# Hybrid encoder block on one core: order of the first row blocks and scales, and GpSimd's share of the beginning moved to VectorE

## The chip, the core and the metric

The kernel runs on one core of a Trainium2 chip. The metric is the device time of one execution in microseconds, from runs of the whole program. The engines of the core, as the profile names them: PE (TensorE, matmuls; PEld its weight loads), DVE (VectorE), ACT (ScalarE), POOL (GpSimd) and SP (SyncE, which here only issues DMAs). Each engine works through its own instructions in the order in which the program gives them, and waits on semaphores where an operand comes from another engine or a DMA.

## The reference

One layer of an encoder block on 1024 tokens of width 1024, in f32. The part that matters here is the beginning:

```python
u = rms_norm(x, norm1_g[l])
proj = u @ w_in[l]
q, k, v, cb, cc, ch, ga, gb = jnp.split(proj, split_pts, axis=-1)
q = rms_norm(q.reshape(B, S, N_HEADS, HEAD_DIM), q_norm_g[l])
k = rms_norm(k.reshape(B, S, N_HEADS, HEAD_DIM), k_norm_g[l])
...
y_a = neighbourhood_attention(q, k, v, rpb[l]) @ w_attn_branch[l]
y_b = short_gated_conv(cb, cc, ch, conv_w[l]) @ w_conv_branch[l]
merged = jax.nn.sigmoid(ga) * y_a + jax.nn.sigmoid(gb) * y_b
x = x + merged @ w_o[l]
h = rms_norm(x, norm2_g[l]) @ w_mlp_in[l]
x = x + jnp.square(jax.nn.relu(h)) @ w_mlp_out[l]
```

V, Q and K have 512 columns each; the row norm is over the 1024 columns of x.

## The kernel before

**Numbers.** Products of f32 matrices are made from f16 halves: an operand is scaled by a power of two, rounded to f16 (the high part) and the rest is rounded again (the low part). A product takes three passes, high by high, high by low and low by high (`PASSES`, L440). So each weight chunk needs a scale, then high parts on ScalarE (L290, a copy with a scale) and low parts (L278 on VectorE, one multiply-and-subtract). For the scale, a chunk is measured once: V's two chunks by the largest magnitude, weighted by the row gain (`largest`, L296, VectorE), the chunks of Q, K, the convolution and the first gate by a sum of squares (L241, ScalarE, the squares themselves go to the place where the low parts will stand) times `gm2`, the squared largest row gain. A matmul with a matrix of ones (`all_sum`, L179) sums over the partitions, and a few 128x1 integer instructions make the power of two (`pow2`, L105, or `pow2_half`, L402).

**Row blocks.** x is eight blocks of 128 rows. `norm` (L414) is a generator, one step per yield: Square with its row sum and a root on ScalarE, four small VectorE instructions (`rstd`), the high half `u` on ScalarE (L420), the low half on VectorE (L422). Blocks 0 to 2 are then turned on TensorE (`ln_trans`: high and low half, each copied out of PSUM, L432 on ScalarE and L434 on VectorE), blocks 3 to 7 by a transposing DMA (`ln_turn`, L437). A turned block is an operand `uT` of every projection.

**Units.** A unit is 24 matmuls into one PSUM bank. `v_unit(b, j, steps, ticks)` (L502) makes half j (256 columns) of V for row block b, or both halves (512 columns) if j is None; its result is taken out later as two f16 halves (L508, L509). Behind a unit, `step` advances the generators of the foreground (`fg`) and `tick` those of the background (`bg`, the weight chunks that are being prepared). `apart` holds a generator back until some units more have been issued; it is a matter of order only. `flush` runs the background to its end.

**V's parts on GpSimd.** V's chunks have two pieces of 4 x 256 columns. The low parts of the first are made on VectorE, those of the second on GpSimd (`pool`): four scalings into f32 (L287), then four subtractions (L276).

**Gate forms.** The gates are computed later by a seven-product scheme. Its operands of the rows are made in this stage by `sforms` (L467), four times, for the block pairs (n, n + 4): two scalings of x on ScalarE (L474), four 512-column sums or differences on GpSimd (L480), the high half on ScalarE (L482, 2048 columns), the low half on VectorE (L484), and a store to DRAM (`sform_store`, L489). The f16 tile `s16` has two buffers, so the third form is written where the first stood until its store had read it. `SFORM` says after which unit each form starts.

**Weight loads.** There are five `raw` buffers. `load_upto` (L212) issues the next load as soon as a piece's low parts have been issued, and the load itself waits on SP's queue until these have run. All DMAs of this stage, loads, transposes and stores, are issued by SP in one order.

**The order.** The calls from L514 to L561 are written out by hand: which norm step, which tick and which unit come when. The loop `for p in range(11)` issues the rest of V (p 1 to 5 halves, p 6 to 10 whole blocks 3 to 7) and the norms of the later blocks; at p = 3 Q's chunk goes into the background. Q's eight units and K's eight follow (L611 on): each result is taken out of PSUM, scaled and normed by head (`qk_vec`: L577, L578 on ScalarE, L581 to L597 on both), and K's weight parts are made during Q's last units.

Of the kernel before, what the change touches and what calls it, by code (L numbers as in the profile page):

```python
# [52 lines left out]
def encoder_block(ctx: ExitStack, tc: tile.TileContext, x, weights, cols, gqk, rel, masks, out):  # L53
# [12 lines left out]
    def bank(tag):  # L66
        return psum.tile([128, 512], F32, name="ps_" + tag, tag=tag, bufs=banks[tag])
# [6 lines left out]
    def anybank():  # L74
        rc[0] += 1
        return bank("dsodsods"[rc[0] % 8])
# [83 lines left out]
    def apart(mark, n=3, of=units):  # L160
        while of[0] < mark + n and not forced[0]:
            yield WAIT
# [15 lines left out]
    def all_sum(a, out, bk, floor, lag=1):  # L178
        T.matmul(bk[:, 0:1], ones[:, 0:128], a, start=True, stop=True)  # L179
        yield  # L180
        yield from apart(units[0], lag)
        V.tensor_scalar(sc[:, out], bk[:, 0:1], floor, None, op0=OP.max)
        yield
# [16 lines left out]
    def settle():  # L200
        while late:
            late.pop(0)()
# [17 lines left out]
    class Chunk:  # L220


        def __init__(self, kind, widths, tag, rows, half, more):
            self.kind, self.bank = kind, {"V": "o", "Q": "o", "K": "s", "C": "d"}.get(kind)
            self.tag, self.rows, self.widths, self.more = tag, rows, widths, more
            self.offs = []
            self.raw, self.ready, self.half, self.pool = [], more > 0, half, () if half is None else (1,)
            self.split = False

        def prep(self):  # L230
            n = len(self.widths)
            nk = sum(k for k, _ in self.widths)
            rm, a, b, s = (cols_of("prep", i) for i in (nk, 1, 1, 1))
            self.inv = keep()
            tot = sum(k * w for k, w in self.widths)
            if self.kind in "QKCG":
                self.parts = wsp.tile([128, 2, tot], F16, name="w16_ws", tag="ws")
                for p, (k, w) in enumerate(self.widths):
                    while len(self.raw) <= p:
                        yield WAIT  # L240
                    A.activation(self.parts[:, 1, :k * w].bitcast(BF16), self.raw[p][:, :k * w], AF.Square,  # L241
                                 accum_out=sc[:, at(rm, p)])
                    yield
                V.tensor_reduce(sc[:, a], sc[:, at(rm, 0, n)], axis=AX, op=OP.add)
                c = ones_col()
                V.tensor_tensor(c, sc[:, a], sc[:, gm2], op=OP.mult)
                yield from apart(units[0], 2 if self.kind == "Q" else 3)
                yield from all_sum(c, b, bank(self.bank) if self.bank else anybank(), 1e-36)
                yield from pow2_half(b, 14, s, self.inv, more=self.more)
            else:  # L250
                yield from self.largest(rm, a, b)
                yield from pow2(b, 14, s, self.inv, False, more=self.more)
            V.tensor_scalar(sc[:, rm], sc[:, self.rows], sc[:, s], None, op0=OP.mult)
            yield
            while done[0] < self.first or self.tag not in wpool:
                yield WAIT
            if self.half is not None:
                if not self.half:
                    vhome.append(wsp.tile([128, 2, 2, tot], F16, name="w16_v", tag="ws"))
                self.parts = vhome[0][:, self.half]  # L260
            elif self.kind not in "QKCG":
                self.parts = wpool[self.tag].tile([128, 2, tot], F16, name="w16_" + self.tag, tag=self.tag)
            f = o = 0
            todo = []
            for p, (k, w) in enumerate(self.widths):
                todo.append((p, [(i * w, w, rm.start + o + i) for i in range(k)], f))
                f += k * w
                o += k
            prev, scaled = None, {}
            for it in todo + [None]:  # L270
                if prev:
                    p, parts, f = prev
                    for o, m, c in parts:
                        hi, lo = (self.parts[:, w, f + o:f + o + m] for w in range(2))
                        if p in self.pool:
                            G.tensor_tensor(lo, scaled[p][:, o:o + m], hi, op=OP.subtract)  # L276
                        else:
                            V.scalar_tensor_tensor(lo, self.raw[p][:, o:o + m], sc[:, c:c + 1], hi,  # L278
                                                   op0=OP.mult, op1=OP.subtract)
                    done[0] += 1  # L280
                    load_upto(done[0] + 5)
                if it:
                    p, parts, f = it
                    if p in self.pool:
                        scaled[p] = w1p.tile([128, 1024], F32, name="scaled", bufs=1)
                        for o, m, c in parts:
                            G.tensor_scalar(scaled[p][:, o:o + m], self.raw[p][:, o:o + m], sc[:, c:c + 1], 1.0,  # L287
                                            op0=OP.mult, op1=OP.mult)
                    for o, m, c in parts:
                        A.activation(self.parts[:, 0, f + o:f + o + m], self.raw[p][:, o:o + m], AF.Copy,  # L290
                                     scale=sc[:, c:c + 1])
                prev = it
                self.split = it is None
                yield
# [129 lines left out]
    def ln_trans(u16, b, dst):  # L424
        for s in range(2):
            pt = bank16("o")
            for k in range(8):
                T.transpose(pt[:, k * 128:(k + 1) * 128], u16[:, s, k * 128:(k + 1) * 128], ident)
            o = dst[:, s, :, b * 128:(b + 1) * 128]
            i = pt.rearrange("p (k t) -> p k t", k=8)  # L430
            if s == 0:
                A.activation(o, i, AF.Copy)  # L432
            else:
                V.tensor_copy(o, i)  # L434
# [27 lines left out]
    GS = dram.tile([128, 4, 4, 2, 512], F16, name="gs")  # L462

    turned, formed = [0], [0]
    SFORM = (6, 8, 10, 12)

    def sforms():  # L467

        for n, start in enumerate(SFORM):
            yield from apart(start, 0)  # L470
            assert turned[0] >= n + 5
            z = []
            for b in (n, n + 4):
                A.activation(xt[:, b], xt[:, b], AF.Copy, scale=sc[:, at(ys, b)])  # L474
                z += [xt[:, b, :512], xt[:, b, 512:]]
            f = wqk.tile([128, 4, 512], F32, name="sform", bufs=1)
            v = wqk.tile([128, 4, 2, 512], F16, name="s16", bufs=2)
            for o, a, b, op in ((2, z[0], z[2], OP.subtract), (0, z[2], z[3], OP.subtract),
                                (1, f[:, 0], z[0], OP.subtract), (3, z[1], f[:, 1], OP.add)):
                G.tensor_tensor(f[:, o], a, b, op=op)  # L480
            yield from apart(start, 2)
            A.activation(v[:, :, 0], f, AF.Copy)  # L482
            yield
            V.tensor_tensor(v[:, :, 1], f, v[:, :, 0], op=OP.subtract)  # L484
            fg.append(sform_store(n, v))
# [6 lines left out]
    def ln_step(b, n=1):  # L492
        for _ in range(n):
            advance(ln[b])
# [17 lines left out]
                               for k in range(8) for sa, sw in PASSES]), post, steps, ticks)  # L512

    push(cV[0])  # L514
    ln_step(0, 2)
    tick()
    ln_step(0, 5)
    ln_step(1)
    tick(3)
    ln_step(0)  # L520
    ln_step(1)
    tick(4)
    ln_trans(u16[:, 0], 0, UT)
    flush()
    ln_step(1, 5)
    ln_step(1)
    ln_step(2, 2)
    push(cV[1])
    tick(1)
    v_unit(0, 0, 0, 0)  # L530
    ln_step(2, 4)
    ln_trans(u16[:, 1], 1, UT)
    ln_step(2, 1)
    tick(3)
    ln_step(2)
    tick(4)
    ln_step(3, 2)
    ln_trans(u16[:, 2], 2, UT)
    ln_step(3, 4)
    fg.append(qk_gain())  # L540
    fg.append(sforms())
    V.tensor_reduce(sc[:, gm2], sc[:, g1], axis=AX, op=OP.max, apply_absolute_value=True)
    mul(gm2, gm2, gm2)
    for p in range(11):
        if p == 3:
            flush()
            push(cQ)
        if 0 < p < 6:
            v_unit(p % 3, p // 3, 1, 2)
        elif p:  # L550
            v_unit(p - 3, None, 2, 4)
        for q in (p,) if p < 6 else (2 * p - 6, 2 * p - 5):
            c = q // 2 + 3
            if c < 8 and q % 2 == 0:
                ln_step(c, 2)
                ln_turn(u16[:, c % 4], c, UT)
                turned[0] = c + 1
            if c < 7:
                ln_step(c + 1, 3)
    settle()  # L560
    flush()  # L561

# [1154 lines left out]
```

## Time and profile before

| | us |
|---|---|
| median of 3 runs | 1249.16 |
| lowest and highest | 1244.13, 1250.89 |
| profiled execution: time | 1249.31 |
| profiled execution: span of the core | 1247.2 |
| mean granted clock of TensorE | 0.992 |

The profile comes from one execution. A row of the timeline is: start, duration, engine, line of the kernel, operation, output<-inputs, shapes, count, and in brackets how long the engine had been idle before it and what released it. Neighbouring instructions of one kind are merged into one row (x24), whose duration runs from the first start to the last end. A row of the stretches is: the stretch, its length, then busy time and count for PE, PEld, DVE, ACT and POOL, the granted TensorE clock, the DMA engines' busy share, and GB/s. A row of the groups is: line, engine, operation, tiles, shapes, count, then busy us in total and mean ns of one, then the idle time before them and what ended it. Rows of one view that stand together are told apart by this form. "DMA to landing" is the time from the issue of a tile's DMAs to their completion.

| engine, whole span | busy us |
|---|---|
| PE | 1203.7 |
| DVE | 929.7 |
| ACT | 765.1 |
| POOL | 438.8 |

### The profile page before, as it was taken

What the parts mean: (1) busy time and instruction counts of PE and PEld (TensorE: products, weight loads), DVE (VectorE), ACT (ScalarE), POOL (GpSimd) and SP (SyncE); (2) the same over time, 40 slices, a digit from 0 to 9 for tenths busy, and PEclk for the clock granted to TensorE, in tenths of its full rate; (3) what the DMA queues carried; (4) which work ended last, traced back from release to release, by engine and by line L of the source; (5) the groups of instructions that cost most, each with busy time, mean ns of one, the idle gap of its engine ahead of it and who ended that gap; (6) DMA issues with size and microseconds to landing.
All of it is one profiled execution on the core that took longest, in us unless ns stands there. A gap on an engine that the chain in (4) does not pass through costs nothing. (4 is left out here: it accounts for less than half of the span.)

```text
span 1247.2 us, 17068 instructions
## 1 busy us (share of the span) xinstructions
PE 1203.7 (97%) x6294; PEld 577.4 (46%) x6294; DVE 929.7 (75%) x1733; ACT 765.1 (61%) x1177; POOL 438.8 (35%) x297
## 2 busy tenths in 40 slices
PE   4989999998999999999998999999999999999998
PEld 3534444554444444444456444444444444444444
DVE  6668778878557686887867655554546999999997
ACT  5777567677464454536665867877855773645430
POOL 2340002221231111101002756556557463373562
PEclk8999999999999999999998999999999999999999
DMA  6458455656552211216185445544575743436202
GB/s 256 105 191 182 79 119 136 130 104 136 122 112 83 68 52 51 68 38 251 59 164 115 155 164 162 186 146 134 186 264 182 272 191 134 173 112 240 101 34 101
DMA packets 170803, 173.35 MB, mean 139 GB/s; under 512 B 131424, under 2 KB 131936, under 8 KB 166624
## 3 DMA queue, kind: packets, MB, share of 16 engines
q1 hardware_dynamic: 170720, 172.27, 46.9%
q8 instruction: 49, 0.80, 0.3%
q14 instruction: 34, 0.28, 0.1%
HBM read 102.51 MB, written 37.75 MB: 112 GB/s over the span
## 5 line engine op out<-in xcount | busy, mean ns | idle before, releaser
L188 PEld LDWEIGHTS <-ops 128*128 128x128 f16 x1356 | 132.4, 98 | 159.3 <-issue 2.4
L188 PEld LDWEIGHTS <-w 128*128 128x128 f16 x1368 | 133.1, 98 | 143.8 <-issue 5.2
L858 PE MATMUL ps_d<-uT,w_ws 128*128 128x512 f16 x528 | 126.5, 382 | 0.0
L188 PE MATMUL ps_d<-ops 128*128 128x512 f16 (+1 forms) x528 | 118.3, 374 | 0.0
L188 PE MATMUL ps_s<-ops 128*128 128x512 f16 x492 | 113.2, 379 | 1.5 <-DVE ops L1550 1.1
L1541 ACT ACTIVATE ops<-hf,sc 128x2048 f16<-128x2048 f32 x26 | 52.0, 1999 | 94.6 <-PE ps_o L188 35.1
L1155 POOL TENSOR_TENSOR as<-as 128x512 f32<-128x512 f32 x64 | 88.0, 1374 | 42.5 <-ACT as L1412 38.7
L188 PEld LDWEIGHTS <-uT 128*128 128x128 f16 x648 | 64.8, 101 | 70.8 <-issue 5.7
L962 POOL TENSOR_TENSOR tsum<-raw 128x512 f32<-128x512 f32 x28 | 47.4, 1709 | 137.0 <-ACT raw L948 137.0
L188 PEld LDWEIGHTS <-w_s 128*128 128x128 f16 x588 | 56.7, 98 | 69.4 <-DVE w_s L973 1.9
L188 PE MATMUL ps_d<-u2x,w 128*128 128x512 f16 (+1 forms) x360 | 80.0, 372 | 0.0
L1543 DVE SCALAR_TENSOR_TENSOR ops<-hf,sc,ops 128x2048 f16<-128x2048 f32 x26 | 73.8, 2838 | 5.2 <-ACT ops L1541 5.2
L188 PE MATMUL ps_o<-ops 128*128 128x512 f16 x336 | 77.1, 379 | 0.0
L858 PEld LDWEIGHTS <-w_ws 128*128 128x128 f16 x528 | 51.2, 98 | 53.5 <-issue 1.7
L188 PE MATMUL ps_o<-u2T,w 128*128 128x512 f16 (+1 forms) x324 | 73.2, 376 | 0.0
L948 ACT ACTIVATE raw<-raw,sc 128x256 f32<-128x256 f32 x172 | 71.1, 493 | 0.9 <-DMA raw<-in_weights 0.9
L962 POOL TENSOR_TENSOR gsum<-raw 128x512 f32<-128x512 f32 x14 | 19.0, 1374 | 131.5 <-issue 57.1
L1436 DVE TENSOR_TENSOR as<-ps_d,as 128x512 f32<-128x512 f32 (+1 forms) x15 | 10.1, 674 | 62.5 <-ACT as L1453 62.5
L977 ACT ACTIVATE w<-raw,sc 128x512 f16<-128x512 f32 (+1 forms) x28 | 24.6, 927 | 52.2 <-DVE sc L410 52.2
L805 ACT ACTIVATE sz<-sz,sc 128x384 f32<-128x384 f32 (+1 forms) x64 | 37.3, 583 | 27.6 <-DVE sc L796 16.2
L188 PE MATMUL ps_s<-u2T,w 128*128 128x512 f16 (+1 forms) x252 | 52.7, 359 | 0.0
L278 DVE SCALAR_TENSOR_TENSOR w_ws<-raw,sc,w_ws 128x512 f16<-128x512 f32 (+2 forms) x72 | 49.0, 733 | 3.7 <-ACT w_ws L290 3.7
(333 smaller groups left out, 2616.3 us busy)
## 6 DMA issues: line engine op xcount, KB each, us to landing
raw<-in_weights SPq DMA_DIRECT2D x89, 512.0 KB, 5.6
hs<-as SPq DMA_DIRECT2D x16, 1792.0 KB, 8.8
hf<-hs SPq DMA_DIRECT2D x26, 1024.0 KB, 6.7
w2x<-in_weights SPq DMA_DIRECT2D x16, 512.0 KB, 8.1
raw<-in_weights SPq DMA_DIRECT2D x16, 384.0 KB, 3.9
xt<-in_x SPq DMA_DIRECT2D x8, 512.0 KB, 10.2
gs<-s SPq DMA_DIRECT2D x4, 1024.0 KB, 6.7
x<-in_x SPq DMA_DIRECT2D x8, 512.0 KB, 9.7
```

What stands on the lines that cost most here:

```text
L188: T.matmul(ps, l, r, start=a, stop=b)
L278: V.scalar_tensor_tensor(lo, self.raw[p][:, o:o + m], sc[:, c:c + 1], hi, op0=OP.mult, op1=OP.subtract)
L805: A.activation(z, z, AF.Exp, scale=-1.0, bias=sc[:, d["mx"]], accum_out=sc[:, d["sm"]])
L858: T.matmul(ps, l, r, start=a, stop=b)
L948: A.activation(v, v, AF.Copy, scale=sc[:, at(g, 4 * i + k)])
L962: G.tensor_tensor(t[:, o], a, b, op=OP.add)
L977: A.activation(o(0), w, AF.Copy, scale=sc[:, s])
L1155: sub.tensor_tensor(z[o], z[a], z[b], op=op)
L1436: V.tensor_tensor(z[5], ps[6], z[4], op=OP.add)
L1541: A.activation(P[:, 1, 0], hf, AF.Copy, scale=sc[:, Rs])
L1543: V.scalar_tensor_tensor(P[:, 1, 1], hf, sc[:, Rs], P[:, 1, 0], op0=OP.mult, op1=OP.subtract)
```

## The change

It touches the beginning only, up to the last block of V. The second chunk of V (`half` = 1) gets its scale from sums of squares, like Q and K, without the waits of order, and writes its squares into its own place in V's tile; `gm2` is therefore made earlier. GpSimd no longer makes low parts of V, and the sums of the gate forms go to VectorE. The written order is changed: norm 0 is finished up to its high half ahead of V's first measurement, norm 1's small instructions come ahead of V's parts, block 1's unit for the first half of V comes before block 2 is turned, and in the last rounds (p 6 to 10) the foreground advances behind the norms instead of behind the unit, with more ticks of the background. The first form starts after unit 7 instead of 6, and its second part one unit sooner.

```diff
@@ class Chunk @@
-            self.raw, self.ready, self.half, self.pool = [], more > 0, half, () if half is None else (1,)
+            self.raw, self.ready, self.half = [], more > 0, half
@@ prep @@
-            if self.kind in "QKCG":
-                self.parts = wsp.tile([128, 2, tot], F16, name="w16_ws", tag="ws")
+            if self.kind in "QKCG" or self.half:
+                self.parts = vhome[0][:, 1] if self.half else wsp.tile([128, 2, tot], F16, name="w16_ws", tag="ws")
...
-                yield from apart(units[0], 2 if self.kind == "Q" else 3)
-                yield from all_sum(c, b, bank(self.bank) if self.bank else anybank(), 1e-36)
+                if not self.half:
+                    yield from apart(units[0], 2 if self.kind == "Q" else 3)
+                yield from all_sum(c, b, bank(self.bank) if self.bank else anybank(), 1e-36, not self.half)
...
-            prev, scaled = None, {}
+            prev = None
...
-                        if p in self.pool:
-                            G.tensor_tensor(lo, scaled[p][:, o:o + m], hi, op=OP.subtract)
-                        else:
-                            V.scalar_tensor_tensor(lo, self.raw[p][:, o:o + m], sc[:, c:c + 1], hi,
-                                                   op0=OP.mult, op1=OP.subtract)
+                        V.scalar_tensor_tensor(lo, self.raw[p][:, o:o + m], sc[:, c:c + 1], hi,
+                                               op0=OP.mult, op1=OP.subtract)
...
-                    if p in self.pool:
-                        scaled[p] = w1p.tile([128, 1024], F32, name="scaled", bufs=1)
-                        for o, m, c in parts:
-                            G.tensor_scalar(scaled[p][:, o:o + m], self.raw[p][:, o:o + m], sc[:, c:c + 1], 1.0,
-                                            op0=OP.mult, op1=OP.mult)
@@ sforms @@
-    SFORM = (6, 8, 10, 12)
+    SFORM = (7, 8, 10, 12)
...
-                G.tensor_tensor(f[:, o], a, b, op=op)
-            yield from apart(start, 2)
+                V.tensor_tensor(f[:, o], a, b, op=op)
+            yield from apart(start, 1)
@@ the written order @@
     push(cV[0])
-    ln_step(0, 2)
+    ln_step(0, 7)
     tick()
-    ln_step(0, 5)
     ln_step(1)
     tick(3)
     ln_step(0)
     ln_step(1)
     tick(4)
     ln_trans(u16[:, 0], 0, UT)
+    ln_step(1, 4)
+    V.tensor_reduce(sc[:, gm2], sc[:, g1], axis=AX, op=OP.max, apply_absolute_value=True)
+    mul(gm2, gm2, gm2)
     flush()
-    ln_step(1, 5)
+    ln_step(1)
     ln_step(1)
     ln_step(2, 2)
     push(cV[1])
-    tick(1)
+    tick(2)
     v_unit(0, 0, 0, 0)
     ln_step(2, 4)
     ln_trans(u16[:, 1], 1, UT)
     ln_step(2, 1)
-    tick(3)
+    tick(1)
+    v_unit(1, 0, 0, 0)
+    tick(7)
     ln_step(2)
-    tick(4)
-    ln_step(3, 2)
+    ln_step(3, 1)
     ln_trans(u16[:, 2], 2, UT)
-    ln_step(3, 4)
+    tick(2)
+    ln_step(3, 5)
     fg.append(qk_gain())
     fg.append(sforms())
-    V.tensor_reduce(sc[:, gm2], sc[:, g1], axis=AX, op=OP.max, apply_absolute_value=True)
-    mul(gm2, gm2, gm2)
     for p in range(11):
         if p == 3:
             flush()
             push(cQ)
-        if 0 < p < 6:
+        if p == 1:
+            step()
+            tick(2)
+        elif p and p < 6:
             v_unit(p % 3, p // 3, 1, 2)
-        elif p:
-            v_unit(p - 3, None, 2, 4)
+        elif p > 5:
+            v_unit(p - 3, None, 0, 4 if p < 7 else 8)
...
                 ln_step(c + 1, 3)
+        if p > 5:
+            step(2)
     settle()
     flush()
```

In the order in which the changed program gives its instructions, SP's DMAs of this stage stand as follows behind the last transposing DMA of `uT`: before, the store of form 0, four weight loads (K's pieces 1 to 3 and the convolution's first), the stores of forms 1 to 3; after, the four weight loads, then the stores of forms 0 to 3.

## The prediction

> **What bounds the kernel now.** The page first: is there one bound, and where is it absent?
>
> ```profile
> span 1247.2 us, 17068 instructions
> PE   4989999998999999999998999999999999999998
> ```
>
> TensorE is the bound almost everywhere; the first three slices (31 us each) are the weak ones. The change touches only instructions up to the first block of K, so I read that stretch in order of time, TensorE first.
>
> ```profile
> 24.36 0.18 PE L179 MATMUL ps_o<-ones 128*128 128x1 bf16 x1 [3.54 <-DVE ones L311]
> 26.45 4.29 PE L188 MATMUL ps_s<-w_v,uT 128*128 128x256 f16 x24
> 36.53 2.78 PE L188 MATMUL ps_s<-w_v,uT 128*128 128x256 f16 x24
> 65.01 5.35 PE L188 MATMUL ps_s<-w_v,uT 128*128 128x512 f16 x24 [2.34 <-DMA uT<-u]
> 75.81 3.24 PE L188 MATMUL ps_d<-w_ws,uT 128*128 128x512 f16 x14 [0.87 <-DVE w_ws L278]
> 78.89 5.34 PE L188 MATMUL ps_o<-w_ws,uT 128*128 128x512 f16 x24
> 115.17 5.34 PE L188 MATMUL ps_d<-w_ws,uT 128*128 128x512 f16 x24
> 120.35 5.34 PE L188 MATMUL ps_o<-w_ws,uT 128*128 128x512 f16 x24
> ...
> 24.00:26.00 2.00, 1.42 (x13) 1.23 (x14) 1.86 (x7) 0.20 (x2) 0.00 (x0) 0.50 0.02 8
> 100.00:120.00 20.00, 20.00 (x95) 9.05 (x93) 18.39 (x49) 15.51 (x26) 1.83 (x2) 1.00 0.76 133
> ```
>
> Three losses stand here: 3.54 us for V's second scale, after which the granted clock is 0.50 and a unit of 24 matmuls takes 4.29 instead of 2.78; 2.34 us for row block 7; and some 3.4 us in Q's first unit, which follows block 7's (65.01 + 5.35), waits for its weight parts until 75.81, and ends when the next begins, at 78.9: 8.5 us for 5.2. From then TensorE never stops, one 512-column unit each 5.18 us (115.17 to 120.35, the first of K). But in 100 to 120 VectorE is busy 18.39 of 20 us: the lead it has there is small, and that decides this case.
>
> **The durations.** One row each for the operations that the change adds, removes or moves (mean of one in ns; POOL's forms row is one of three):
>
> ```profile
> L422 DVE SCALAR_TENSOR_TENSOR u<-xt,sc,u 128x1024 f16<-128x1024 f32 x8 | 11.7, 1461 | 7.0 <-ACT u L420 5.8 <-DMA xt<-in_x 1.2
> L484 DVE TENSOR_TENSOR s<-sform,s 128x2048 f16<-128x2048 f32 x4 | 9.2, 2288 | 8.1 <-ACT s L482 8.1
> L301 DVE TENSOR_REDUCE sc<-raw 128x4 f32<-128x1024 f32 x4 | 4.9, 1215 | 0.7 <-DMA raw<-in_weights 0.6
> L509 DVE SCALAR_TENSOR_TENSOR vT<-ps_s,vT 128x512 f16<-128x512 f32 x3 | 2.0, 679 | 0.0
> L588 DVE TENSOR_TENSOR qs<-qs,sc 128x512 f32<-128x512 f32 x2 | 1.4, 686 | 0.0
> L420 ACT ACTIVATE u<-xt,sc 128x1024 f16<-128x1024 f32 x8 | 9.2, 1144 | 5.3 <-DVE sc L399 5.2
> L474 ACT ACTIVATE xt<-xt,sc 128x1024 f32<-128x1024 f32 x8 | 8.7, 1134 | 0.0
> L241 ACT ACTIVATE w_ws<-raw 128x1024 bf16<-128x1024 f32 x8 | 8.4, 1048 | 0.1
> L480 POOL TENSOR_TENSOR sform<-xt 128x512 f32<-128x512 f32 x8 | 11.4, 1446 | 26.6 <-ACT xt L474 11.6 <-ACT w_ws L241 6.1 <-DVE s L484 4.4
> 12.54 3.29 ACT L290 ACTIVATE w_v<-raw,sc 128x256 f16<-128x256 f32 x8
> 13.27 2.57 DVE L278 SCALAR_TENSOR_TENSOR w_v<-raw,sc,w_v 128x256 f16<-128x256 f32 x4
> 36.23 1.28 DVE L422 SCALAR_TENSOR_TENSOR u<-xt,sc,u 128x1024 f16<-128x1024 f32 x1 [0.64 <-ACT u L420]
> 32.07 1.67 DVE L278 SCALAR_TENSOR_TENSOR w_v<-raw,sc,w_v 128x256 f16<-128x256 f32 x4
> 113.98 1.40 DVE L278 SCALAR_TENSOR_TENSOR w_ws<-raw,sc,w_ws 128x512 f16<-128x512 f32 x2
> ...
> DMA to landing us min/median/max: 4.2/4.3/4.4
> ```
>
> With GpSimd busy beside it a low part of V took 0.64 (2.57/4); with GpSimd quiet 0.42 (1.67/4), a low half of a norm 1.28, and a low part of Q or K 0.70 (1.40/2). A high part of V takes 0.41 (3.29/8). The last row is the transposing DMA of a row block: 4.3.
>
> **The change, part by part.** *V's first scale.* Its first maximum (1.2 us) moves behind block 0's norm, which is then 0.9 us earlier; but the second maximum waits for its load as before, and so does the scale: 0. *GpSimd's half of V's low parts* goes to VectorE: 4 x 0.42 = 1.7 us more per half of V; GpSimd loses 8 subtractions and 8 scalings, which were off the path. *V's second scale*: two Squares of 1.05 and 0.19 for reading the sum on ScalarE (2.4 us) instead of two maxima of 1.2 on VectorE: 0 in sum, but they now stand before the copy of the turned block 1, which comes 0.9 us later: ScalarE has eight high parts from 12.54 to 15.8, then the high half of norm 1 (16.9) and a Square (18.1); VectorE has six small instructions more ahead of V's low parts (14.3), eight of these (17.6) and the low half of norm 1 (18.8), before which ScalarE can't go on; then the two Squares of V (2 x 1.17) end at 21.3, and the copy at 22.3. Its unit can still start near 22.5 instead of 26.45, because the scale's small matmul no longer stands ahead of it with 3.54 us of waiting. That gain isn't kept. The next unit needs turned block 2. On ScalarE: high half of norm 2 and a PSUM copy to 23.6; VectorE's copy and seven small instructions, V's scale, to 25.1; four high parts to 26.7, a Square to 27.8, and the copy of block 2, done at 28.8, where that unit began at about 30.6 (behind the 4.29). 1.8 us are left.
>
> From there the two vector engines hand the work to and fro, and TensorE follows. I walk the new order with the rows above, small instructions at 0.19 and a ScalarE copy at 0.3 to 0.5. Four high parts and the last low part of V: 30.9. Six small ones, high and low half of norm 3 (1.15 + 1.28): 34.5. Small ones and a copy (1.3), norm 4 (2.4): 38.2. Two copies and Q's four Squares (5.4), norm 5 (2.4): 46.0. Copies and small ones (2.1), norm 6 (2.4): 50.5. A root and two scalings of x (2.3): 52.9. Then *the four sums of the first gate form, now on VectorE* (4 x 0.63 = 2.5; POOL took over 5) to 55.45; a copy, and norm 7 to 57.3. Block 7 then lands at 61.6 (4.3 after its low half). The 512-column sum of two f32 tiles isn't in the trace on VectorE: between a quarter of L484 (0.57) and L588 (0.69); I take 0.63, and eight of them lie on this path: 0.5 us either way. Then VectorE has low form 0 (to 59.7), form 1's sums (62.2), a copy, and Q's scale, done at 63.9. High parts and high form 1 on ScalarE to 68.2; low form 1 on VectorE 2.3, a copy 0.6, and the last six of Q's eight low parts, 6 x 0.70, end at 75.3. Q's first unit ends at 75.9 instead of 78.9: **3.0 us gained**, if what follows keeps up.
>
> *What follows* is the point of this forecast. In the new order the store of gate form 0 stands on SP's queue behind four weight loads. Each load waits for low parts of Q, since those free its buffer. Before:
>
> ```profile
> 62.69 0.99 SPq L489 DMA_DIRECT2D gs<-s  x1
> 72.42 6.33 SPq L210 DMA_DIRECT2D raw<-in_weights  x4
> 78.81 13.31 SPq L489 DMA_DIRECT2D gs<-s  x3
> ...
> 66.47 2.29 DVE L484 TENSOR_TENSOR s<-sform,s 128x2048 f16<-128x2048 f32 x1 [3.83 <-ACT s L482]
> ...
> DMA to landing us min/median/max: 4.6/4.6/4.6
> ...
> DMA to landing us min/median/max: 8.6/8.6/8.6
> ...
> 75.23 1.91 ACT L482 ACTIVATE s<-sform 128x2048 f16<-128x2048 f32 x1 [0.32 <-POOL sform L480]
> 82.39 0.67 ACT L577 ACTIVATE qs<-ps_d,sc 128x512 f32<-128x512 f32 x1
> 87.52 1.91 ACT L482 ACTIVATE s<-sform 128x2048 f16<-128x2048 f32 x1 [1.99 <-DMA gs<-s]
> 94.23 0.67 ACT L577 ACTIVATE qs<-ps_d,sc 128x512 f32<-128x512 f32 x1
> 110.24 0.67 ACT L577 ACTIVATE qs<-ps_d,sc 128x512 f32<-128x512 f32 x1
> 111.47 0.71 ACT L290 ACTIVATE w_ws<-raw,sc 128x512 f16<-128x512 f32 x1
> 117.38 1.40 DVE L278 SCALAR_TENSOR_TENSOR w_ws<-raw,sc,w_ws 128x512 f16<-128x512 f32 x2
> ```
>
> Store 0 went at 62.69, ahead of the loads, and landed in 4.6 us. Store 1, whose data was ready at 68.8, went only at 78.81, behind them, and took 8.6; ScalarE lost 1.99 us to it at 87.52. The forms have two buffers, so form 2 waits for store 0. Afterwards store 0 is ready at 59.7 but goes behind the fourth load, at 75.3 + 0.4 = 75.7, into the company that store 1 had: I take 8.6, so 84.3 (the other end is 4.6, 4.0 us sooner). [...]
>
> So form 2's high half, at 75.23 before, starts at 84.3, and ScalarE and VectorE are in order behind it: 1.8 for it, 0.5 copy, 2.1 two scalings, 3.5 three Squares of K (1.17 each), 1.9 high form 3, 2.3 low form 3: 96.4. After that Q's second block is taken from PSUM 1.2 later, the third one cycle of 4.0 on (a quarter of the 16.0 below): 101.6, against 94.23. Third to seventh block took 110.24 - 94.23 = 16.0, with VectorE full, so none of it is made good: K's high parts begin at 101.6 + 16.0 + 1.2 = 118.8 against 111.47, **7.3 later**. K's last low part moves from 118.8 (117.38 + 1.40) to 126.1, and its first unit ends two matmuls on, at 126.5 instead of 120.35: 6.15 later. TensorE, done with Q at about 114.5, stands idle nearly 5 us before K. A gap of 3.54 gave clock 0.50 and 1.5 us per unit (4.29 less 2.78); here the parts set half the pace, so I add 0.8, ends 0 and 3.0 (twice 1.5, for twice the columns). [...]
>
> Sum: span 1247.2, with 2.1 around it the profiled run's 1249.3 (the median shown is 1249.16), + 6.15 + 0.8 = 1256.3, **1256**. After K's first unit TensorE goes on without holes as before, so nothing gives it back.
>
> **The rivals.** *Hidden, and not slower.* If store 0 had landed by 77.8, when VectorE has form 2's sums ready, it would decide nothing; everything behind it would come 6.5 sooner, K's first unit would end at 120.0, 0.35 early, and without the hole: 1249. If VectorE's cycle of 4.0 were also shorter with GpSimd quiet, Q's 3.0 would stay: 1246. For it: TensorE reaches Q 3 us sooner, and the data of store 0 is ready at 59.7. Against: the loads stand ahead of the store, and 94.23 to 110.24 was run with POOL nearly idle already (1.83 of 20 us). *Slower still.* Store 1 leaves 0.4 us behind store 0 and shares its engines; company cost the old store 1 4.0 us (8.6 less 4.6), and if the two interleave, another 1 MB comes in, which I price at 3: ScalarE waits to 87, and with the clock's 3.0 the sum is 1256.3 + 3.0 + 2.2 = 1261.5. Store 1's 8.6, with store 2 only 2.4 behind it, speaks half for it. *It doesn't do what it says*: the scale of V "at once" gains nothing if the Squares push the copy of block 1 past 22.5; TensorE has slack there, so 0 on the end.
>
> **How the numbers follow.** Forecast (store 0 lands 82 to 86, 1252.5 to 1259): 0.60. Slower still (to 1262): 0.17. Hidden or landing in 4.6 (1246 to 1252.5): 0.23. Range: 1256.3 less 4.0, 0.5 and 0.8 is 1251.0, and 3.0 + 2.2 + 0.5 more is 1262.0; with a little for runs, 1250 to 1262. A measurement tells 0.5%, 6.2 us, from no change: 1255.4 and above is slower. That is all of the second case and two thirds of the first: 0.58. Faster (below 1242.9) needs more than all of Q's gain: 0.06. Same: 0.36.
>
> **What would show it.** Right: form 2's high half preceded by several us of idle "DMA gs<-s"; the first eviction of Q near 94; a hole of 4 to 6 us on TensorE before K's first unit, with clock 0.5. Early steps: block 1's unit near 22.5, block 7's near 61.6, Q's first unit done near 76. Wrong: no DMA wait on ScalarE, or K's first unit at 115 without a hole; then 1246 to 1249. If low parts of Q end later than 75.3, everything behind moves by as much.

## The result and the profile after

| | before | after |
|---|---|---|
| median, us | 1249.34 | 1253.44 |
| lowest and highest of 20 runs | 1243.56, 1251.69 | 1249.87, 1256.93 |
| ratio to before, 95% interval | | 1.0038 [1.0027, 1.0050] |
| profiled execution: time | 1249.31 | 1254.62 |
| profiled execution: span | 1247.2 | 1252.7 |

The change costs 4.1 us by the medians. That is below the 0.5% that the prediction set as the bound of what can be told from no change, though with 20 runs on each side the interval lies above 1. The time is in the predicted range, 2.6 us under the number. In the comparisons further below, one run of the kernel before that took 3203.73 us is left out.

The page of the kernel after, the span and TensorE's busy tenths in 40 slices:

```profile
span 1252.7 us, 17055 instructions
...
PE   4988999999999999999998999999999999999998
```

Two slices differ from the page of before: the fourth (94 to 125 us), now 8 and not 9, and the tenth (282 to 313 us), now 9 and not 8. The rest has to be read from the timeline. TensorE of the kernel after:

```profile
22.13 2.79 PE L188 MATMUL ps_s<-w_v,uT 128*128 128x256 f16 x24 [0.35 <-ACT uT L425]
61.38 5.34 PE L188 MATMUL ps_s<-w_v,uT 128*128 128x512 f16 x24
72.00 5.53 PE L188 MATMUL ps_d<-w_ws,uT 128*128 128x512 f16 x17 [3.77 <-DVE w_ws L276]
77.37 5.34 PE L188 MATMUL ps_o<-w_ws,uT 128*128 128x512 f16 x24
...
108.48 5.34 PE L188 MATMUL ps_o<-w_ws,uT 128*128 128x512 f16 x24
118.87 0.58 PE L188 MATMUL ps_d<-w_ws,uT 128*128 128x512 f16 x1 [5.05 <-ACT w_ws L283]
119.93 7.07 PE L188 MATMUL ps_d<-w_ws,uT 128*128 128x512 f16 x23 [0.48 <-DVE w_ws L276]
126.83 5.34 PE L188 MATMUL ps_o<-w_ws,uT 128*128 128x512 f16 x24
```

Two stretches of the same kernel; the third number from the end is TensorE's granted clock:

```profile
74.00:76.00 2.00, 2.00 (x6) 0.64 (x5) 2.00 (x4) 0.00 (x0) 0.00 (x0) 0.50 0.76 281
118.00:120.00 2.00, 0.66 (x2) 0.17 (x2) 2.00 (x5) 2.00 (x5) 0.00 (x0) 0.50 0.00 0
```

The front does what the change says: block 1's unit of V starts at 22.13 instead of 26.45, block 7's at 61.38 instead of 65.01 and without its wait for the transpose, Q's second unit at 77.37 instead of 78.89. Then the lead is lost: TensorE has no work from 113.8 to 118.87, and K's second unit begins at 126.83 instead of 120.35, 6.48 late. TensorE's longest wait behind its first matmuls was the 3.54 at V's second scale before; now it is the one in front of K.

What made K's parts late is on the three other engines. The kernel after: SP's queue, then ScalarE, then VectorE in the timeline.

```profile
66.21 9.41 SPq L210 DMA_DIRECT2D raw<-in_weights  x4
75.67 20.42 SPq L482 DMA_DIRECT2D gs<-s  x4
...
64.01 2.56 ACT L283 ACTIVATE w_ws<-raw,sc 128x512 f16<-128x512 f32 x4 [4.34 <-DVE sc L254]
83.74 1.91 ACT L475 ACTIVATE s<-sform 128x2048 f16<-128x2048 f32 x1 [9.88 <-DMA gs<-s]
100.67 0.67 ACT L577 ACTIVATE qs<-ps_d,sc 128x512 f32<-128x512 f32 x1
116.87 0.67 ACT L577 ACTIVATE qs<-ps_d,sc 128x512 f32<-128x512 f32 x1
118.11 2.54 ACT L283 ACTIVATE w_ws<-raw,sc 128x512 f16<-128x512 f32 x4
...
57.14 2.29 DVE L477 TENSOR_TENSOR s<-sform,s 128x2048 f16<-128x2048 f32 x1 [0.18 <-ACT s L475]
71.21 4.05 DVE L276 SCALAR_TENSOR_TENSOR w_ws<-raw,sc,w_ws 128x512 f16<-128x512 f32 x6
124.01 1.40 DVE L276 SCALAR_TENSOR_TENSOR w_ws<-raw,sc,w_ws 128x512 f16<-128x512 f32 x2
```

Form 0 is complete at 59.4 (57.14 + 2.29), and its store stands on SP's queue until 75.67, behind four loads that wait for Q's low parts (done at 75.26). Form 2's high half waits 9.88 us for it. Everything behind on ScalarE is late with it: the form's high half by 8.5 us (before: 75.23), K's high parts by 6.6 (118.11 against 111.47). "Evictions" are the instructions that take a unit's result out of PSUM.

### The profile page after: what moved, and what is told of

It is laid out like the page before. It is cut to its first block, busy times and chain, and to the rows that moved or that the text cites. A ratio compares the mean times of both kernels' runs of the same rounds, so it can differ in the third digit from the quotient of the medians.

```text
span 1252.7 us, 17055 instructions
## 1 busy us (share of the span) xinstructions
PE 1203.9 (96%) x6294; PEld 577.0 (46%) x6294; DVE 932.7 (74%) x1756; ACT 767.2 (61%) x1181; POOL 408.3 (33%) x265
## 4 chain that ended last, share of the span: by engine, by line
PE 38%; DVE 6%; ACT 4%; issue 2%; DMA 1%; DVEq 0%; SPq 0%; ACTq 0%
PE ps_d L188 15%; PE ps_s L188 13%; PE ps_o L188 10%; DVE ops L1550 1%; DVE v L1195 1%; DMA u2x<-v 1%; DVE w L973 1%; ACT as L1410 1%; DVE form L1155 0%; ACT w L977 0%; ACT raw L948 0%; DVE ops L1543 0%; ACT as L1412 0%; ACT ops L1541 0%; DVE x L1324 0%
## 5 line engine op out<-in xcount | busy, mean ns | idle before, releaser
L188 PE MATMUL ps_o<-u2T,w 128*128 128x512 f16 (+1 forms) x324 | 73.2, 376 | 0.0
L188 PE MATMUL ps_d<-w_ws,uT 128*128 128x512 f16 x192 | 46.9, 403 | 9.3 <-ACT w_ws L283 5.0
L572 POOL TENSOR_TENSOR biasm<-bias,mk 128x384 f32<-128x384 f32 x8 | 7.3, 914 | 141.2 <-DVE sc L401 111.1
```

Source lines behind the costliest of these rows:

```text
L188: T.matmul(ps, l, r, start=a, stop=b)
```

## The experiments

Two theories. **S**: the store's place on SP's queue, behind the loads, makes ScalarE wait, and this alone turns a lead into a loss. **D**: the form sums, four for each of four forms, some 11 us of new work for VectorE (16 of 0.69), make the chain before K longer; the wait for the store is only where the slack shows. All kernels were compared with the kernel before on the same chip.

The table sets the start of K's second unit in the profile of each (before: 120.35) beside the difference of the medians.

| kernel | K's second unit starts, us | span from there, us | median less before's | ratio, 95% interval |
|---|---|---|---|---|
| before | 120.35 | 1126.9 | | |
| after | 126.83 | 1125.9 | +4.1 | 1.0038 [1.0027, 1.0050] |
| after, store at once | 120.08 | 1122.0 | -0.4 | 0.9995 [0.9979, 1.0011] |
| after, loop undone | 120.14 | 1124.5 | +0.7 | 1.0013 [0.9999, 1.0027] |
| before, loop alone | 122.97 | 1126.8 | +2.8 | 1.0023 [1.0010, 1.0037] |
| after, sums on GpSimd | 131.60 | 1126.1 | +12.1 | 1.0101 [1.0072, 1.0130] |
| store at once, K's parts earlier | 118.54 | 1127.0 | -3.0 | 0.9981 [0.9964, 0.9998] |
| the same, form 2 on GpSimd | 120.48 | 1127.0 | -1.7 | 0.9988 [0.9975, 1.0001] |
| after, clock kept | 126.02 | 1124.9 | +2.6 | 1.0019 [1.0005, 1.0033] |

In six of the eight edits the medians stay within 2.0 us of what this one start says (its difference from 120.35); in the other two, after and after with the clock kept, they are 2.4 and 3.0 below it, and only a part of this is explained, for after (last section). The part behind it, 1122 to 1127 us in profiles of kernels that have the same work there, is the noise on which all this is measured.

**The store at once.** The store of a form is issued with its low half and not one unit later, so it stands ahead of the loads.

```diff
-            fg.append(sform_store(n, v))
+            SP.dma_start(GS[:, n], v)
+            formed[0] = n + 1
```

> The changed kernel with one edit: a gate form's store is issued as soon as its low half is, not a unit later, so that store 0 stands ahead of the four weight loads on SP's queue; the other engines keep their orders. Theory S (the loss is store 0 queued behind the loads): store 0 lands near 64, form 2's high half starts near 78 (VectorE's sums decide) instead of 83.7, no DMA wait of over 1 us on ScalarE, K's first unit ends about 5.5 to 6.5 us sooner, no hole of over 2 us before it, and the time falls by 5 to the old kernel's: 1249, ratio 1.000, 0.997 to 1.002. Rival D (the loss is VectorE's 10 us more work for the form sums): ratio stays at 1.003 to 1.005.

Measured 1247.6, ratio 0.9995. SP, ScalarE and TensorE of this kernel, then the landing of its four stores:

```profile
59.34 0.49 SPq L478 DMA_DIRECT2D gs<-s  x1
66.08 0.33 SPq L210 DMA_DIRECT2D raw<-in_weights  x1
...
77.88 1.91 ACT L475 ACTIVATE s<-sform 128x2048 f16<-128x2048 f32 x1 [4.15 <-issue]
112.30 2.54 ACT L283 ACTIVATE w_ws<-raw,sc 128x512 f16<-128x512 f32 x4
...
120.08 5.34 PE L188 MATMUL ps_o<-w_ws,uT 128*128 128x512 f16 x24
```

```profile
DMA to landing us min/median/max: 3.8/4.1/4.8
```

The store goes at 59.34, every store lands within 4.8 us, form 2's high half starts 5.86 sooner (77.88 against 83.74; the 4.15 before it is marked "issue", and VectorE has form 2's sums ready just then, at 77.8), K's high parts 5.81 sooner, and the hole is gone. VectorE has the same work as in the kernel after. All four stores moved, but the kernel after has only one wait for a store on ScalarE, the 9.88 us for store 0. So D falls as the cause of the loss, and S holds: the place of that one DMA decides. But it leaves no gain either: Q's lead is spent before K, because the chain of ScalarE and VectorE brings K's parts at 112.30 (before: 111.47).

**The loop undone.** The order of the loop over p is put back as before, all other parts of the change are left in.

```diff
-            v_unit(p - 3, None, 0, 4 if p < 7 else 8)
+            v_unit(p - 3, None, 2, 4)
...
-        if p > 5:
-            step(2)
```

> The changed kernel with the loop over V's last blocks as before (two steps and four ticks behind each unit, none behind the norms); scales, V's parts and form sums as changed. Store 0 goes ahead of the loads again. S: no wait for store 0; ratio 0.997 to 1.002. D: 1.003 or more, since VectorE still has the sums.

Measured 1248.74, ratio 1.0013. TensorE, and one stretch of the same kernel:

```profile
21.82 2.78 PE L188 MATMUL ps_s<-w_v,uT 128*128 128x256 f16 x24
65.33 8.32 PE L188 MATMUL ps_s<-w_v,uT 128*128 128x512 f16 x24 [3.62 <-DMA uT<-u]
120.14 5.34 PE L188 MATMUL ps_o<-w_ws,uT 128*128 128x512 f16 x24
```

```profile
66.00:68.00 2.00, 2.00 (x6) 0.73 (x5) 1.93 (x6) 0.00 (x0) 0.00 (x0) 0.50 0.51 209
```

V's scale at once starts V's second unit at 21.82, and yet block 7's unit starts at 65.33, later than before (65.01): the gain of the first 30 us ends in a longer wait for block 7's transpose (3.62 against 2.34), and a cold clock behind it (granted at 0.50; 8.32 for 5.35). The early parts of the change, without the loop, are worth nothing at the end. For the two theories the run speaks as S says: store 0 goes at 63.00, ahead of the loads, ScalarE has no wait for a store, and the ratio's interval ends below D's 1.003, though VectorE has all the sums.

**The loop alone.** The reverse: the kernel before with only the new loop order (its `sforms` still runs its sums on GpSimd).

```diff
-            v_unit(p - 3, None, 2, 4)
+            v_unit(p - 3, None, 0, 4 if p < 7 else 8)
...
+        if p > 5:
+            step(2)
```

> The kernel before with that loop change alone; form sums and half of V's low parts stay on GpSimd. Store 0 goes behind the loads. S: form 2's high half waits for the store to about 82 (75.2 before), a hole before K's first unit, 1252 to 1256, ratio 1.002 to 1.006. D: VectorE has no more work than before, so 1249 or less, ratio 1.000.

Measured 1250.85, ratio 1.0023, in S's range at its low end; form 2 was expected at about 82 and came at 77.95. SP, VectorE, ScalarE and TensorE:

```profile
69.83 23.24 SPq L489 DMA_DIRECT2D gs<-s  x4
65.38 4.05 DVE L278 SCALAR_TENSOR_TENSOR w_ws<-raw,sc,w_ws 128x512 f16<-128x512 f32 x6
77.95 1.91 ACT L482 ACTIVATE s<-sform 128x2048 f16<-128x2048 f32 x1 [6.29 <-DMA gs<-s]
103.36 5.34 PE L188 MATMUL ps_o<-w_ws,uT 128*128 128x512 f16 x24
114.39 0.58 PE L188 MATMUL ps_d<-w_ws,uT 128*128 128x512 f16 x1 [5.69 <-ACT w_ws L290]
```

The loop puts the store behind the loads with none of the rest of the change. Here Q's low parts are done sooner, so the loads and the store go sooner (69.83), and the wait is 6.29 instead of 9.88. TensorE is done with Q at 108.5 (103.36 and one unit of 5.2), 5.3 sooner than after, and waits 5.69 for K's parts. VectorE in the kernel after, where Q's low parts end only at 75.26 and not at 69.43 (65.38 + 4.05):

```profile
59.53 1.30 DVE L473 TENSOR_TENSOR sform<-xt 128x512 f32<-128x512 f32 x2
61.59 0.69 DVE L473 TENSOR_TENSOR sform<-xt,sform 128x512 f32<-128x512 f32 x1
68.40 2.29 DVE L477 TENSOR_TENSOR s<-sform,s 128x2048 f16<-128x2048 f32 x1 [2.22 <-ACT s L475]
```

Two things stand ahead of Q's low parts there that don't with the loop alone: form 1's four sums, ahead of Q's scale (59.53 to 62.28), and form 1's high and low half, ahead of the last six low parts. The last of the four loads waits for Q's low parts, and the store stands behind it. So the rest of the change adds 3.9 us at K's second unit (126.83 against 122.97) to what the loop costs, and VectorE's new work is a part of it: D is wrong about the cause, but that work makes the wait longer. TensorE is done with Q 6.6 us sooner here than before (108.5 against 115.2). What the loop alone would give with the store at once was not run; it is an open question whether more of this lead could be kept than in the versions below.

**The form sums on GpSimd.** The kernel after with the sums where they were before.

```diff
-                V.tensor_tensor(f[:, o], a, b, op=op)
+                G.tensor_tensor(f[:, o], a, b, op=op)
```

> The changed kernel with the form sums on GpSimd again, SP's order as changed. S: store 0 is still behind the loads, ScalarE waits for it 5 us or more, ratio 1.003 to 1.007. D: the loss is gone, ratio 1.000 or less.

Measured 1260.12, ratio 1.0101: the wrong way for D, and beyond S's range. GpSimd, then SP, VectorE and ScalarE:

```profile
74.97 3.28 POOL L473 TENSOR_TENSOR sform<-xt 128x512 f32<-128x512 f32 x2 [7.03 <-ACT xt L467]
80.00 1.26 POOL L473 TENSOR_TENSOR sform<-xt,sform 128x512 f32<-128x512 f32 x1
...
79.20 21.54 SPq L482 DMA_DIRECT2D gs<-s  x4
72.72 6.07 DVE L276 SCALAR_TENSOR_TENSOR w_ws<-raw,sc,w_ws 128x512 f16<-128x512 f32 x6
86.38 1.91 ACT L475 ACTIVATE s<-sform 128x2048 f16<-128x2048 f32 x1 [11.01 <-DMA gs<-s]
```

The four sums of form 2 take 6.3 us (74.97 to 81.26) here, against 2.7 on VectorE (four times 0.69), 2.3 times as long. It isn't these sums that form 2 waits for, but again the store, which goes at 79.20, 3.5 later than after's, and form 2 at 86.38, 2.6 later. The store is later because the loads wait for Q's low parts: Q's scale comes 1.0 later, and the last six low parts take 6.07 us of VectorE, while GpSimd works beside it from 74.97 on, and end at 78.79; after's six took 4.05. Form 3 then waits another 1.89 us for GpSimd's sums. So with the forms in this order, the sums on VectorE start K's second unit 4.8 us sooner than the sums on GpSimd (126.83 against 131.60).

**K's parts earlier.** The edit of the store at once, and with it K's scale one unit of Q earlier, so that K's parts lie one eviction earlier on ScalarE and VectorE.

```diff
-                    yield from apart(units[0], 2 if self.kind == "Q" else 3)
+                    yield from apart(units[0], 2 if self.kind in "QK" else 3)
```

> The changed kernel with the store issued at once, and K's scale asked for one block of Q earlier (its small matmul before Q's fourth unit instead of its fifth), so that K's weight parts are made one eviction of Q earlier. Theory: with the store out of the way, what spends Q's lead is the chain of ScalarE and VectorE (one block of Q per 3.9 us, then K's parts at 112.3), so TensorE, done with Q at 118.7 less 5.2 = 113.5, waits for K's parts; K's first unit ended at 120.08 there and 120.35 before. With the parts one block sooner it starts at 113.5 without waiting and the next at 118.7: 1.4 us less than with the store alone, ratio to before 0.996 to 0.999. Rival: the parts only change places with the evictions of Q, which then come late and hold TensorE's next K units or PSUM banks: K's second unit begins at 120 or later, ratio 0.999 to 1.002.

Measured 1245.97 (before: 1248.99), ratio 0.9981 [0.9964, 0.9998]. ScalarE and TensorE:

```profile
107.88 2.54 ACT L283 ACTIVATE w_ws<-raw,sc 128x512 f16<-128x512 f32 x4
113.19 5.52 PE L188 MATMUL ps_d<-w_ws,uT 128*128 128x512 f16 x24
118.54 5.34 PE L188 MATMUL ps_o<-w_ws,uT 128*128 128x512 f16 x24
```

K's parts begin 4.4 sooner, TensorE goes from Q to K without a hole, and K's second unit begins at 118.54, as expected (118.7). So it was K's parts on which Q's lead was lost, and 1.8 us of the lead now reach K's second unit (before: 120.35). The medians differ by 3.0, and the interval only just leaves 1 out, so that this kernel is faster than before is shown only barely.

**Form 2's sums on GpSimd**, on top of that.

```diff
-                V.tensor_tensor(f[:, o], a, b, op=op)
+                (G if n == 2 else V).tensor_tensor(f[:, o], a, b, op=op)
```

> As the run before it, and the sums of the third gate form on GpSimd again. ScalarE waited 4.15 us for form 2 with the store at once (until 77.88), since VectorE came to its sums only behind Q's low parts (75.05). On GpSimd four sums take some 5.2 to 6.7 us from the time the form's buffer is free (70.5), so 75.7 to 77.2: form 2 goes 0.7 to 2.2 us sooner. Theory: from 77 on TensorE is the bound, and only an earlier end of the chain before K could show: no more than 0.5 us against the run before it, ratio 0.996 to 0.999. Rival: VectorE's 2.7 us of sums were still what the evictions of Q wait for: ratio 0.994 to 0.996.

Measured 1247.3, ratio 0.9988 [0.9975, 1.0001]: the ratio is in the theory's range, the interval reaches above it and leaves the rival's out. GpSimd and ScalarE:

```profile
73.29 3.27 POOL L473 TENSOR_TENSOR sform<-xt 128x512 f32<-128x512 f32 x2 [72.22 <-ACT xt L467]
78.32 1.27 POOL L473 TENSOR_TENSOR sform<-xt,sform 128x512 f32<-128x512 f32 x1
...
79.62 1.91 ACT L475 ACTIVATE s<-sform 128x2048 f16<-128x2048 f32 x1 [5.93 <-POOL sform L473]
```

The expected 0.7 to 2.2 us sooner didn't come: form 2 goes at 79.62, later than with VectorE (77.53 in the run before it), since the sums wait for ScalarE's scaling of x (done at 73.2) and not only for the buffer (70.5), and then take 6.3 us (73.29 to 79.59 on GpSimd). This is a miss of the expectation. Form 2's 2.1 us come back at K's high parts (109.98 against 107.88), Q's second unit starts 1.4 later (78.33 against 76.90), and K's second unit 1.9 later (120.48 against 118.54). Beside GpSimd, the 17 matmuls of Q's first unit that wait for VectorE's low parts took 6.66 us (from 71.84), against 5.53 in the run before it (from 71.53), and the only difference between the two kernels is where form 2's sums run. The times of the two kernels are not told apart by their intervals.

**The clock kept.** The kernel after with 23 matmuls that nobody reads, in the hole before K.

```diff
+        if n == 8:
+            keepup = bank("s")
+            for i in range(23):
+                T.matmul(keepup, UT[:, 0, 0, :128], UT[:, 0, 0, :512], start=i == 0, stop=i == 22)
```

> The changed kernel with 23 extra 128x512 matmuls, whose result nobody reads, behind the last unit of Q, where TensorE waited 5.05 us for K's parts; nothing else is moved. Theory: the wait stays what ScalarE and VectorE make it (K's second unit at 126.83 at best as early as the last low part, 125.4, and two matmuls, 125.9), and the 23 matmuls (23 x 0.216 = 5.0 us) keep the granted clock at 1.00, so K's first unit no longer runs behind its parts: K's second unit starts at 125.8 to 126.1, 0.7 to 1.0 us sooner. Rival: the clock costs nothing there, the parts alone set the pace: 126.6 to 127.0. Ratio to before 1.002 to 1.004 by either, since what the clock does later in the kernel differs by a microsecond from run to run.

Measured 1251.63, ratio 1.0019 [1.0005, 1.0033], just under the range given for both theories (1.002 to 1.004). TensorE, and one stretch of the same kernel:

```profile
113.72 5.13 PE L617 MATMUL ps_s<-uT 128*128 128x512 f16 x23
126.02 5.34 PE L188 MATMUL ps_o<-w_ws,uT 128*128 128x512 f16 x24
```

```profile
118.00:120.00 2.00, 1.23 (x5) 0.39 (x4) 2.00 (x5) 2.00 (x4) 0.00 (x0) 1.00 0.02 4
```

The granted clock stays at 1.00 where it was 0.50, and K's second unit begins at 126.02 instead of 126.83, though K's parts come 0.1 later: the cold clock (granted at 0.50) cost 0.8 to 0.9 us there. The whole time falls more than that, 1.5 us less above before than the kernel after; the intervals overlap, and no more than the 0.8 is shown to come from the edit.

## Why the prediction was right, and where it was off

**The front.** Block 1's unit at 22.5 (measured 22.13) and not kept; block 7's unit without its wait at 61.6 (61.38); Q's scale at 63.9 (ScalarE goes on at 64.01); Q's last low part at 75.3 (71.21 + 4.05 = 75.26). All within 0.4. That the front by itself gives nothing is shown by the loop undone.

**Q's first unit** was to end at 75.9, and the next one began at 77.37: 3.0 us of lead were forecast, 1.5 came. The step that failed is "3.0 us gained": it let the unit end with its last low part. But TensorE had waited 3.77 for the low parts and ran at clock 0.50 (74 to 76), so that 17 matmuls took 5.53 and went on behind the parts. The prediction counted a cold clock before K and not here. The 1.5 us cost nothing at the end: TensorE stood idle for K's parts behind Q anyway (113.8 to 118.87).

**The hole.** TensorE was to be done with Q at about 114.5 and to stand idle nearly 5 us; it was done at 113.8 and stood 5.05, at clock 0.50, and the first eviction of Q began at 93.32 (forecast: near 94). But 114.5 doesn't follow from the prediction's own rows: seven more units of 5.18 behind 75.9 end at 112.2, and the hole would have been some 7 us. That its length came out is luck. The sum doesn't rest on it, since K's first unit was timed by K's parts.

**The store** at 75.7 (75.67), landing 8.6 later at 84.3: form 2's high half started at 83.74, so 8.1 at most. With the store at once the four stores took 3.8 to 4.8 us. The store's wait was the term that decided, and the two experiments on either side, the store at once (wait gone, ratio 0.9995) and the loop alone (wait of 6.29 brought in, ratio 1.0023), show it. How late the store goes depends on when Q's low parts end, and the prediction had that to 0.1 us.

**What follows** went step by step, 0.5 to 0.9 early, as the store was: third block of Q at 100.67 (101.6), K's high parts at 118.11 (118.8), K's last low part ended at 125.41 (126.1). The 16.0 from third to seventh block measured 16.2 (116.87 - 100.67), so VectorE made nothing good. K's second unit was forecast at 126.5 + 0.8 = 127.3 and began at 126.83. The 0.8 for the clock was right in size (0.8 to 0.9).

**The sum.** 1256.3 against the profiled 1254.62. 0.5 of the 1.7 is K's start, 1.0 the rest of the kernel (1252.7 - 126.83 = 1125.9 against 1126.9 before), and 0.2 what lies around the span. "Nothing gives it back" is where the sum was off: the profile of after ran its rest 1.0 us shorter. The rows of the last section show where: before lost about a microsecond to a fallen clock near 208 us, and after did not. This lies behind all that the change touches; whether it is chance or follows from the later start was not shown. The median of after lies another 1.2 below its profiled run, while before's median and profiled run agree; which of the runs a profile happens to be was not in the sum. Beyond this, why the medians differ by only 4.1 and K's start by 6.48 stays open.

**The rivals.** *Hidden* is what the kernel does with the store at once, and the number given for it, K's first unit ending at 120.0 and 1249, was 120.08 and 1247.6 (0.4 us under before; forecast: 0.35). *Slower still* didn't happen: store 1 behind store 0 didn't make ScalarE wait to 87, and the 3 us that the prediction priced for another 1 MB came from no row. *It doesn't do what it says* didn't hold for V. The chances for a large loss were placed too high: 0.58 was given to a loss above 6.2 us, and the loss is 4.1, inside the forecast's own case and on the other side of the bound.

## What to carry to other kernels

A DMA queue that one engine issues in order, as SP's here (store 0 was complete at 59.4 and went at 75.67, behind four loads), is part of the dependency graph: when work is moved, look at which waiting transfer each store comes to stand behind, and who waits for the buffer that the store frees. A lead won in the front of a kernel reaches the end only if the chain of the other engines up to the next weight set is also early: here 3.6 us at block 7's unit was worth nothing until K's parts were moved as well, and then 1.8 us at K's second unit. Issuing a store as soon as its data is there is an edit of two lines and gave back the whole loss.

## What was not expected of the hardware

The clock was cold after waits of 3.62, 3.77 and 5.05 us in the rows above (granted at 0.50 in the stretch beside each), but after two waits of a little over 2 us it was not the same. Of before, then of after, TensorE behind a wait of nearly equal length later in the kernel, with a row that follows a little later, and each with the stretch that holds the wait:

```profile
206.68 0.90 PE L839 MATMUL ps_o<-PT,vT 128*64 128x128 f16 x18 [2.13 <-DMA PT<-P]
210.78 0.49 PE L782 MATMUL ps_s<-kD,qD 128*128 128x384 f16 x2
```

```profile
205.00:210.00 5.00, 3.33 (x25) 1.68 (x25) 2.14 (x8) 4.35 (x14) 0.00 (x0) 0.70 0.43 81
```

```profile
213.22 0.69 PE L839 MATMUL ps_o<-PT,vT 128*64 128x128 f16 x18 [2.18 <-DMA PT<-P]
215.92 0.48 PE L782 MATMUL ps_s<-kD,qD 128*128 128x384 f16 x2
```

```profile
210.00:215.00 5.00, 2.82 (x29) 1.53 (x28) 2.07 (x8) 5.00 (x14) 0.00 (x0) 1.00 0.64 117
```

After 2.13 us the clock fell (0.70 in the mean of the stretch), after 2.18 it stayed at 1.00, with TensorE even less busy. After is 6.54 us late at the first row and 5.14 at the second; some 100 us on (300.24 in before, 305.74 in after) it is 5.50 late, as at the end (1252.7 against 1247.2). So in this pair of profiles the fallen clock is where after's later part became shorter. Why the clock fell after the one wait and not after the other was not shown. Whether the fallen clock is the source of the whole spread of 1122 to 1127 us in the rest of the kernel was not shown: the shortest, with the store at once, had a mean granted clock of 0.996 (before 0.992, after 0.990), but the mean clock doesn't put all of them in order (after has 0.990 and 1125.9, before 0.992 and 1126.9).
